# Causal part of the forgetting masks added on GpSimd behind the output gate, on diagonal blocks only, with the gate's factor made during the projection and a new order of the A/C stage

## The chip, the cores and the metric

The program runs on one core of a Trainium2 chip. The time is the device time of one execution in microseconds (us), from launch to end, the median of several runs. The core has five engines with a queue of instructions each: TensorE (PE in the profile, PEld for its weight loads), VectorE (DVE), ScalarE (ACT), GpSimd (POOL) and SyncE (SP), which here only issues the weight transfers. ACT's queue issues a few small transfers too. Engines wait for each other through semaphores, and every engine runs its own queue in order.

## The reference

Two layers of a decoder trunk on 256 tokens of width 1024, all in float32. Each layer is a half-step SwiGLU FFN, a mixer, and another half-step FFN. The mixer projects the normed tokens once and splits the result into three head groups that attend in parallel: A (4 query heads on one shared key head, keys chosen by an indexer's top 64), B (4 heads, plain causal at this length) and C (8 heads, with a bias from a cumulative forget gate, and a sigmoid output gate). Group C is what the change touches:

```python
def forgetting_attention(q, k, v, log_f):
    c = jnp.cumsum(log_f, axis=1).transpose(0, 2, 1)
    ...
        s = jnp.einsum('bqhd,bkhd->bhqk', qb, k).astype(jnp.float32) * scale
        s = s + cq[..., None] - c[:, :, None, :]
        s = jnp.where((key_pos[None, :] <= qpos[:, None])[None, None], s, -jnp.inf)
        p = jax.nn.softmax(s, axis=-1).astype(v.dtype)
...
    o_c = forgetting_attention(cq, ck, cv.reshape(B, S, C_HEADS, HEAD_DIM), log_f)
    o_c = o_c * jax.nn.sigmoid(cg)
    return jnp.concatenate([o_a, o_b, o_c], axis=-1) @ w_out
```

The term of a query's own row (`cq`) cancels in the softmax, so the kernel adds only the key's term.

## The kernel before

Tokens lie in two tiles of 128 partitions. To keep float32 accuracy on a faster matmul type, each weight is split in a high part (ACT, L123, a cast) and a low part (DVE, L127, a subtraction); `W.pump` records one such pair, and a product is three matmuls (`mm3`, all on L309). A split that is finished frees its raw buffer, and SP then issues the next 1 MB of weights (L97).

**The mixer** first runs the projection: eight column chunks (`CHUNKS`: iq, ib, b, a, ck, cq, cv, cg), each summed in two PSUM banks of the pool `gu` (four banks). Between the chunks' steps, `run_side` records the work that was put on a list with `at_step(n, ...)`: rotary, norms, the indexer's scores, top-k rounds, and the whole of group B. The last chunk, cg, holds the output gate. At step 32 the mask of group A (`amask`, L851 to L855, DVE) is made from the top-k scores. Group C's norms (`c_norm`, L707, four products of 128x512 on POOL) are recorded at step 25.

**The masks of group C** are four tiles of two heads each, `fmask[0..3]`, 128 x (2 x 384): a query tile's key columns are laid out as block 0 (query tile 0, keys 0 to 127), block 1 (query tile 1, keys 0 to 127) and block 2 (query tile 1, keys 128 to 255). Each is filled by a transfer that copies the heads' row of cumulated gates to all partitions (`spread`, L893, on ACT's queue); then `add_causal(j)` (L897, POOL) adds the tile `causal`, which is -1e30 above the diagonal in blocks 0 and 2 and zero in block 1. The first two lie in a tile named fmask, the third in gmask, the fourth in `spare`, a buffer that becomes free only when the projection has read its last input. `spare` holds also the gate `sg` and `cT`, group C's transposed queries and keys. The adds for j = 0, 1, 2 are recorded at step 28, the fourth at the end of `post_cg`.

**The gate**: `post_cg` makes `hr` = half the token norm (L1005, DVE, a 128x2 instruction), then the tanh of each token tile from the cg banks with `hr` as its scale (L1011, ACT), issues the fourth `spread`, and lets POOL turn tanh into a sigmoid (L1014, two instructions).

**The A/C stage** follows the projection. Its order is written out in `AC_ORDER`; each word records one step for all engines, so it sets the order in every queue:

- `c`, `C`, `g`, `G` + j: PE transposes queries and keys of C's head pair j (4 transposes, L1188) into a bank and ACT (small letter) or DVE (capital) copies it to `cT` (L1189). c and C use banks of the pool `acc`, g and G use `gu` banks.
- `s` + i: PE's scores of head pair i (0 and 1 are group A, 2 to 5 are C) into two `gu` banks.
- `m` + i: DVE adds the mask and finds the row's minimum (L1048, two pieces, each with a short read of its result); heads 0 to 3 are A, 4 to 11 are C, so m4 and m5 read fmask[0], m6 and m7 fmask[1], m8 and m9 gmask, m10 and m11 spare.
- `e`: ACT's exponentials (L1059). `d`: DVE divides by the row sum (L1065 and two L1067; group A only). `f`, `F`: PE's three transposes of the probabilities (L1072), copied by ACT or DVE (L1074).
- `v`, `o`: values (PE) and outputs to be projected. `h`: half of one block of the output projection, six matmuls. `w`: one weight split.

The stage ends where `tail` transposes the new trunk for the next norm (L344).

Of the kernel before, what the change touches and what calls it, by code (L numbers as in the profile page):

```python
# [10 lines left out]
F32 = mybir.dt.float32  # L11
# [3 lines left out]
ALU = mybir.AluOpType  # L15
# [3 lines left out]
P = 128  # L19
# [16 lines left out]
DOWN_LAG = 4  # L36
OUT_TAIL = 3
AC_ORDER = """
c0 C1 s0 s1 m1 h m0 e1 e0 m2 e2 c3 m3 d0 d1 h s2 d2 m4 s3 h e3 e4 f1 m6 h f0 m7 f2 m5 d3 f3 F4 e5 v0
v1 o0 G2 o1 e6 F5 h s4 e7 s5 m8 m9 e8 m10 h m11 e9 f6 v2 F7 f9 h w F8 e11 w o2 h e10 v3 F11 v4 f10 h  # L40
o4 o3 w v5 w h w
""".split()
HALVES_AHEAD = 2
WARM = 6
BRIDGE = 3
B_TURN, A_ROPE, B_STEP, A_ROOT, A_TURN, SUMS_STEP, MASK_STEP, ADD_STEP = 18, 18, 20, 22, 27, 23.7, 27.5, 28


CHUNKS = [
# [98 lines left out]
def kernel(ctx: ExitStack, tc: tile.TileContext, x, ffn1_norm, ffn1_w_gate, ffn1_w_up, ffn1_w_down,  # L148
# [9 lines left out]
    sm = ctx.enter_context(tc.tile_pool(name="sm", bufs=4))  # L158
# [6 lines left out]
    V, A, G, T = nc.vector, nc.scalar, nc.gpsimd, nc.tensor  # L165
# [131 lines left out]
    causal = cp.tile([P, 3 * P], F32, name="causal")  # L297
# [379 lines left out]
    def mixer(l, norm, nxt):  # L677
# [3 lines left out]
        def at_step(n, fn):  # L681
            side.append((n, next(count), fn))
# [7 lines left out]
        def heads(ap, n):  # L690
            return ap.rearrange("p (h d) -> p h d", h=n)
# [33 lines left out]
        def evac(dst, ps, t, scale=None):  # L725
            A.activation(dst, ps, AF.Copy, scale=norm.r[:, t:t + 1])
# [21 lines left out]
        st = {}  # L748
# [17 lines left out]
        def post_ib(ps):  # L766
# [119 lines left out]
            at_step(MASK_STEP, mask_tiles)  # L886
            at_step(SUMS_STEP, cumsum)
            at_step(SUMS_STEP + 1, forget_rows)
            at_step(ADD_STEP, lambda: [add_causal(j) for j in range(3)])

        def spread(m, h):
            rows_ = st["fd"][h:h + m.shape[1]]
            A.dma_start(m, bass.AP(tensor=rows_.tensor, offset=rows_.offset, ap=[[0, P]] + list(rows_.ap)))  # L893

        def add_causal(j):
            m = st["fmask"][j]
            G.tensor_tensor(m, m, causal[:, None, :].to_broadcast([P, 2, 3 * P]), op=ALU.add)  # L897

        def post_a(ps):
            ss = sm.tile([P, 2, 5], F32, name="ssa", tag="ss")  # L900
# [98 lines left out]
        def post_cv(ps):  # L999
            for t in range(2):  # L1000
                evac(va[t][:, :, 0:64], heads(ps[t], 8), t)

        def post_cg(ps):
            hr = sm.tile([P, 2], F32, name="hr", tag="hr")
            V.tensor_scalar(hr, norm.r, 0.5, None, op0=ALU.mult)  # L1005
            spare = xp.tile([P, 4096], F32, name="spare", tag="xhl")
            st["cT"] = spare[:, :2048].rearrange("p (h c s) -> p h c s", h=4, c=2)
            sg = spare[:, 2048:3072].rearrange("p (t d) -> p t d", t=2)
            st["fmask"].append(spare[:, 3072:3840].rearrange("p (h c) -> p h c", h=2))
            for t in range(2):  # L1010
                A.activation(sg[:, t], ps[t], AF.Tanh, scale=hr[:, t:t + 1])  # L1011
            spread(st["fmask"][3], 6)
            for t in range(2):
                G.tensor_scalar(sg[:, t], sg[:, t], 0.5, 0.5, op0=ALU.mult, op1=ALU.add)  # L1014
            add_causal(3)
            st["sg"] = sg


# [118 lines left out]

        oT = {}
        posts = dict(iq=post_iq, ib=post_ib, a=post_a, b=post_b, ck=post_ck, cq=post_cq, cv=post_cv, cg=post_cg)
        for name, cols in CHUNKS:  # L1140
            n = sum(c[1] for c in cols)
            ps = [bank("gu") for _ in range(2)]
            for u in range(4):
                w = W.take()
# [38 lines left out]
        def c_T(j, copy, b=None):  # L1183

            b = bank("gu") if b is None else b
            for c, src in enumerate((cq, ck)):
                for t in range(2):
                    T.transpose(b[:, c * S + t * P:c * S + (t + 1) * P], src[t][:, 2 * j:2 * j + 2], ident)  # L1188
            copy(cT[:, j], b.rearrange("p (c s) -> p c s", c=2))  # L1189

        def qk_ac(kind, h):
            if kind == "A":
# [4 lines left out]
        scores, masks, exps, divide, flip, values, outT = run_heads(hs, qk_ac, "gu")  # L1197
        run = dict(h=lambda i: next(halves), w=lambda i: W.pump(), m=masks, e=exps, d=divide,
                   s=lambda i: scores(2 * i), f=flip, F=lambda i: flip(i, V.tensor_copy),
                   c=lambda i: c_T(i, A.copy, acc[2 + i % 2]), C=lambda i: c_T(i, V.tensor_copy, acc[2 + i % 2]),  # L1200
                   g=lambda i: c_T(i, A.copy), G=lambda i: c_T(i, V.tensor_copy),
                   v=lambda i: values(2 * i + 1) if i < 2 else [values(2 * i + e) for e in range(2)],
                   o=lambda i: outT(i)())
        for word in AC_ORDER:
            run[word[0]](int(word[1:] or 0))
        return tail(acc, oT, OUT_ORDER[8 - OUT_TAIL:], 1.0, nxt, lambda: outT(len(hs) // 2 - 1)())
# [2 lines left out]
    def before_mixer(l):  # L1209
        if l == 0:  # L1210
            V.memset(causal[:, P:2 * P], 0.0)
            for t in range(2):
                V.tensor_scalar(causal[:, 2 * t * P:(2 * t + 1) * P], future, NEG, None, op0=ALU.mult)
        mixer_tables(l)
# [8 lines left out]
    norm = Norm(0, 0)  # L1223
    turn_gains()
    for l in range(DEPTH):
        norm = ffn(norm, lambda: Norm(1, l), lambda: before_mixer(l), l == 0)
        norm = mixer(l, norm, lambda: Norm(2, l))
        norm = ffn(norm, (lambda: Norm(0, l + 1)) if l + 1 < DEPTH else None)
# [35 lines left out]
```

## Time and profile before

| | |
|---|---|
| median of 3 runs | 1031.35 us (1031.28 to 1031.7) |
| the profiled execution's own time | 1029.86 us |
| its span, first to last instruction | 1027.5 us |
| mean granted TensorE clock | 0.997 |
| DVE busy | 809.1 us (79%) |
| ACT busy | 582.7 us (57%) |
| POOL busy | 161.5 us (16%) |
| A/C stage, layer 1: 284.61 (first L1188) to 328.85 (L344) | 44.24 us |
| A/C stage, layer 2: 793.72 to 837.96 | 44.24 us |

The page's rows give busy time as an average over the span. A row of a timeline has the start in us from the span's first instruction, the duration in us, the engine, the line, the operation, output<-inputs, the shape and the count of instructions merged; a bracket at its end is the idle time of the engine before it and who ended that. A matmul's duration overlaps its successor's, so PE's times are taken from one start to the next. Other engines' successive starts overlap by about a tenth of a microsecond too.

### The profile page before, as it was taken

The page shows a single profiled execution, that of the slowest core. Times are in us where ns is not written, and L with a number is a line of the kernel's source. Part 1 is how long each engine was busy: PE and PEld are TensorE (multiplying, and loading weights), DVE is VectorE, ACT ScalarE, POOL GpSimd, SP SyncE. Part 2 cuts the span into 40 slices and gives each one's busy share as a digit, 9 for nine tenths or more (in the row PEclk, how much of TensorE's full clock was granted, in tenths as well). Part 3 has the DMA queues.
Part 4 walks back from the last instruction along what each step waited for, and adds up shares of the span by engine and source line. Part 5 has one row for each costly group of instructions (what it writes and reads, how often), then busy time and mean ns, then how long its engine had stood idle before and what let it go on. Part 6 is the DMA issues. An engine that isn't in the chain of part 4 may idle for free.

```text
span 1027.5 us, 14846 instructions
## 1 busy us (share of the span) xinstructions
PE 1016.6 (99%) x5524; PEld 872.8 (85%) x5524; DVE 809.1 (79%) x1516; ACT 582.7 (57%) x1048; POOL 161.5 (16%) x185
## 2 busy tenths in 40 slices
PE   9999999999989999999999999999999999999998
PEld 8888888888868888888888888888887788888887
DVE  6978778789977877777888777787899778777776
ACT  6655555667645655555465555556775555555552
POOL 2003000166820000000000110002678100000000
PEclk9999999999999999999999999999999999999999
DMA  9674656555622464645645564755456134464731
GB/s 325 222 246 159 214 184 198 177 197 180 226 82 83 136 233 152 218 170 206 198 164 191 186 216 152 246 178 184 165 201 214 57 124 159 169 217 153 239 130 41
DMA packets 131703, 184.77 MB, mean 180 GB/s; under 512 B 7152, under 2 KB 104752, under 8 KB 131632
## 3 DMA queue, kind: packets, MB, share of 16 engines
q1 hardware_dynamic: 130704, 180.66, 52.2%
q10 hardware_dynamic: 928, 3.18, 1.0%
q8 instruction: 43, 0.70, 0.3%
q14 instruction: 28, 0.23, 0.1%
HBM read 182.75 MB, written 1.07 MB: 179 GB/s over the span
## 4 chain that ended last, share of the span: by engine, by line
PE 96%; DVE 3%; issue 0%; ACT 0%; POOL 0%; DVEq 0%; ACTq 0%; POOLq 0%
PE ps_gu L309 63%; PE ps_acc L309 29%; DVE wl L127 2%; PE ps_acc L344 1%; PE ps_gu L1072 1%; DVE amask L853 0%; PE ps_acc L738 0%; DVE amask L851 0%; DVE score L846 0%; DVE m L844 0%; PE ps_acc L1072 0%; ACT spare L1011 0%; PE ps_gu L1115 0%; PE ps_acc L506 0%; PE ps_gu L1188 0%
## 5 line engine op out<-in xcount | busy, mean ns | idle before, releaser
L127 DVE TENSOR_TENSOR wl<-raw,wh 128x1024 fp32r<-128x1024 f32 (+2 forms) x342 | 421.6, 1243 | 25.2 <-ACT wh L123 25.1
L123 ACT CAST wh<-raw 128x1024 fp32r<-128x1024 f32 (+2 forms) x341 | 342.4, 1036 | 12.9 <-PE ps_gu L309 11.0
L309 PE MATMUL ps_gu<-xhl,wh 128*128 128x512 f32 x1408 | 330.2, 390 | 0.3 <-DVE xhl L336 0.3
L309 PEld LDWEIGHTS ps_gu<-xhl,wh 128*128 128x128 f32 x1408 | 262.8, 188 | 54.1 <-issue 0.4
L309 PEld LDWEIGHTS ps_gu<-xhl,wl 128*128 128x128 f32 x1408 | 175.8, 192 | 4.1 <-DVE wl L490 0.2
L309 PE MATMUL ps_gu<-xhl,wl 128*128 128x256 f32 x1408 | 178.7, 284 | 0.0
L309 PE MATMUL ps_gu<-wh,xhl 128*128 128x512 f32 (+2 forms) x512 | 156.8, 379 | 0.0
L453 DVE TENSOR_TENSOR tmp<-ps_gu,tmp 128x256 f32<-128x256 f32 x176 | 72.9, 423 | 106.4 <-ACT tmp L452 106.2
L309 PE MATMUL ps_acc<-wh,hh 128*128 128x512 f32 (+1 forms) x352 | 137.3, 390 | 0.0
L309 PE MATMUL ps_acc<-wl,hh 128*128 128x512 f32 (+1 forms) x352 | 137.1, 389 | 0.0
L309 PE MATMUL ps_acc<-wh,hl 128*128 128x512 f32 (+1 forms) x352 | 136.6, 388 | 0.0
L452 ACT COPY tmp<-ps_gu 128x256 f32<-128x256 f32 x176 | 63.4, 371 | 92.1 <-PE ps_gu L309 91.8
L309 PEld LDWEIGHTS ps_gu<-wh,xhl 128*128 128x128 f32 x512 | 94.8, 188 | 16.2 <-issue 1.3
L467 ACT CAST hh<-tmp 128x256 fp32r<-128x256 f32 x80 | 32.6, 407 | 119.5 <-DVE tmp L464 119.5
L309 PE MATMUL ps_gu<-wl,xhl 128*128 128x512 f32 (+2 forms) x256 | 95.7, 374 | 0.0
L459 ACT ACTIVATE tmp<-tmp 128x256 f32<-128x256 f32 x88 | 36.8, 419 | 83.6 <-DVE tmp L457 83.2
L320 POOL TENSOR_TENSOR y_n<-msq,minus_half 128x2 f32<-128x2 f32 x6 | 7.0, 1168 | 491.4 <-DVE msq L319 491.4
L309 PEld LDWEIGHTS ps_acc<-wh,hl 128*128 128x128 f32 x352 | 66.2, 188 | 13.8
L309 PEld LDWEIGHTS ps_acc<-wh,hh 128*128 128x128 f32 x352 | 66.3, 188 | 12.6
L309 PEld LDWEIGHTS ps_acc<-wl,hh 128*128 128x128 f32 x352 | 66.3, 188 | 12.1
L309 PEld LDWEIGHTS ps_gu<-wl,xhl 128*128 128x128 f32 x256 | 48.2, 188 | 6.9
L333 ACT ACTIVATE xhl<-ps_acc,gT 128x256 fp32r<-128x256 f32 x48 | 19.0, 475 | 38.1 <-PE ps_acc L344 35.6
(230 smaller groups left out, 949.3 us busy)
## 6 DMA issues: line engine op xcount, KB each, us to landing
raw<-in_ffn_w_down_dram SPq DMA_DIRECT2D x44, 1024.0 KB, 5.0
raw<-in_ffn_w_gate_dram SPq DMA_DIRECT2D x42, 1024.0 KB, 6.6
raw<-in_ffn_w_up_dram SPq DMA_DIRECT2D x42, 1024.0 KB, 7.4
raw<-in_w_in_dram SPq DMA_DIRECT2D x24, 1024.0 KB, 5.2
raw<-in_w_out_dram SPq DMA_DIRECT2D x8, 1024.0 KB, 4.9
raw<-in_w_in_dram SPq DMA_DIRECT2D x4, 768.0 KB, 5.0
raw<-in_w_in_dram SPq DMA_DIRECT2D x4, 656.0 KB, 4.2
raw<-in_ffn_w_gate_dram SPq DMA_DIRECT2D x3, 512.0 KB, 6.4
```

What stands on the lines that cost most here:

```text
L123: self.nc.scalar.copy(hv, src)
L127: (engine or self.nc.vector).tensor_tensor(lv, self.srcs[self.n_low], hv.bitcast(F32), op=ALU.subtract)
L309: T.matmul(o, l, r, start=start, stop=stop, skip_group_check=True)
L320: G.tensor_tensor(y, dst, minus_half[:, :n], op=ALU.pow)
L333: A.activation(self.h[:, m], src, AF.Copy, scale=gT[:, self.col + m:self.col + m + 1])
L344: T.transpose(ps[:, i, t * P:(t + 1) * P], trunk[:, t, (2 * mp + i) * P:(2 * mp + i + 1) * P], ident)
L452: A.copy(o, ps[:, 1])
L453: V.tensor_tensor(o, ps[:, 0], o, op=ALU.add)
L459: A.activation(th, t_, AF.Tanh, scale=0.5)
L467: (V.tensor_copy if late else A.copy)(hh, t_)
L1072: T.transpose(b[:, j * P:(j + 1) * P], pj[i][:, j * P:(j + 1) * P], ident)
```

## The change

Four edits, the same in both layers. (1) `hr` is made at step 24 of the projection, not in `post_cg`. (2) The three adds of step 28 and the one of `post_cg` are taken out there and become words of the A/C order, `a0` to `a3`. (3) Each add works on blocks 0 and 2 alone, with a pattern of four dimensions, 512 elements of a partition where it was 768. (4) `AC_ORDER` is new. The old table began `c0 C1 s0 s1 m1 h m0 e1 e0 m2 e2 c3 m3 d0 d1 h s2 d2 m4 s3 h`; the new one is in the diff, with the `a` words in it.

```diff
+G3 C1 c0 s0 s1 m0 a0 h a3 e0 a2 m2 m3 m1 e2 h e1 d2 d0 e3 g2 d1 d3 s2 h m4 m5 f1 f0 e4 e5 h F2 F3 s4
+v0 m8 m9 a1 v1 o0 o1 f4 w s3 e8 e9 s5 h m10 h m7 m6 m11 F5 F8 e6 f9 v2 F6 h e11 e7 e10 f7 o2 v4 f10
...
-            at_step(ADD_STEP, lambda: [add_causal(j) for j in range(3)])
...
         def add_causal(j):
-            m = st["fmask"][j]
-            G.tensor_tensor(m, m, causal[:, None, :].to_broadcast([P, 2, 3 * P]), op=ALU.add)
+            m = st["fmask"][j].rearrange("p h (b c) -> p h b c", b=3)[:, :, 0:3:2]
+            both = causal.rearrange("p (b c) -> p b c", b=3)[:, None, 0:3:2].to_broadcast([P, 2, 2, P])
+            G.tensor_tensor(m, m, both, op=ALU.add)
...
+        hr = sm.tile([P, 2], F32, name="hr", tag="hr")
+        at_step(24, lambda: V.tensor_scalar(hr, norm.r, 0.5, None, op0=ALU.mult))
+
         def post_cg(ps):
-            hr = sm.tile([P, 2], F32, name="hr", tag="hr")
-            V.tensor_scalar(hr, norm.r, 0.5, None, op0=ALU.mult)
...
-            add_causal(3)
+            st["add"] = add_causal
...
-                   o=lambda i: outT(i)())
+                   o=lambda i: outT(i)(), a=st["add"])
```

POOL's queue at the end of layer 1's projection, before (-) and after (+); the first rows are group C's norms, the L1014 or L1015 rows the gate:

```order
 L707 TENSOR_TENSOR ck_130<-ck_130,y_c 128x512
 L707 TENSOR_TENSOR cq_128<-cq_128,y_c 128x512
-L897 TENSOR_TENSOR fmask<-fmask,causal 128x768 x2
-L897 TENSOR_TENSOR gmask<-gmask,causal 128x768
-L1014 TENSOR_SCALAR spare<-spare 128x512 x2
-L897 TENSOR_TENSOR spare<-spare,causal 128x768
+L1015 TENSOR_SCALAR spare<-spare 128x512 x2
+L897 TENSOR_TENSOR fmask<-fmask,causal 128x2x2x128
+L897 TENSOR_TENSOR spare<-spare,causal 128x2x2x128
+L897 TENSOR_TENSOR gmask<-gmask,causal 128x2x2x128
+L897 TENSOR_TENSOR fmask<-fmask,causal 128x2x2x128
```

The three adds that stood ahead of the gate now stand behind it, in the order fmask[0], spare, gmask, fmask[1]; the second of them needs the last transfer.

DVE's queue at the same place, before; `amask` is group A's mask, `ps_acc` the bank of C1:

```order
L127 TENSOR_TENSOR wl<-raw,wh 128x1024
L851 TENSOR_SCALAR amask<-score_2310 128x128
L853 SCALAR_TENSOR_TENSOR amask<-score_2309,cst 128x128
L853 SCALAR_TENSOR_TENSOR amask<-score_2310,cst 128x128
L855 TENSOR_SCALAR amask<-amask 128x384
L127 TENSOR_TENSOR wl<-raw,wh 128x1024
L1005 TENSOR_SCALAR hr<-y_n 128x2
L1189 COPY spare<-ps_acc 128x512
L1048 ISA tmp,nm<-ps_gu,amask,minus_a 128x128
```

And after; the row with `ps_gu` is G3's copy:

```order
L127 TENSOR_TENSOR wl<-raw,wh 128x1024
L851 TENSOR_SCALAR amask<-score_2311 128x128
L853 SCALAR_TENSOR_TENSOR amask<-score_2310,cst 128x128
L853 SCALAR_TENSOR_TENSOR amask<-score_2311,cst 128x128
L855 TENSOR_SCALAR amask<-amask 128x384
L127 TENSOR_TENSOR wl<-raw,wh 128x1024
L1190 COPY spare<-ps_gu 128x512
L1190 COPY spare<-ps_acc 128x512
L1049 ISA tmp,nm<-ps_gu,amask,minus_a 128x128
```

`hr` is gone from this place, and G3's copy stands there.

PE's queue after, at its first transposes of probabilities: the last three transposes of g2, s2 (`spare`), the third h (`wh,oh` opens each of its halves), and f1 with f0 (L1073):

```order
L1189 MATMUL ps_gu<-ident,cq_128 128x128
L1189 MATMUL ps_gu<-ident,ck_129 128x128
L1189 MATMUL ps_gu<-ident,ck_130 128x128
L309 MATMUL ps_gu<-spare 128x128 x2
L309 MATMUL ps_gu<-spare 128x256 x2
L309 MATMUL ps_acc<-wh,oh 128x512
L309 MATMUL ps_acc<-wl,oh 128x512
L309 MATMUL ps_acc<-wh,ol 128x512
L309 MATMUL ps_acc<-wh,oh 128x512
L309 MATMUL ps_acc<-wl,oh 128x512
L309 MATMUL ps_acc<-wh,ol 128x512
L1073 MATMUL ps_gu<-ident,p 128x128 x6
```

Ahead of them stand twelve transposes (G3, C1, c0), s0, s1 and two h; before, there were eight transposes (c0, C1) ahead of s0. With G3 in a `gu` bank, the two banks of s0 are now one that the chunk cv left and the one that G3's copy leaves, and the two of s1 are those of the gate. Before, s0 had cv's two banks and s1 the gate's two.

More of the change, by code (lines that the diff above doesn't have):

```diff
@@ L38 @@
 AC_ORDER = """
-c0 C1 s0 s1 m1 h m0 e1 e0 m2 e2 c3 m3 d0 d1 h s2 d2 m4 s3 h e3 e4 f1 m6 h f0 m7 f2 m5 d3 f3 F4 e5 v0
-v1 o0 G2 o1 e6 F5 h s4 e7 s5 m8 m9 e8 m10 h m11 e9 f6 v2 F7 f9 h w F8 e11 w o2 h e10 v3 F11 v4 f10 h
-o4 o3 w v5 w h w
+G3 C1 c0 s0 s1 m0 a0 h a3 e0 a2 m2 m3 m1 e2 h e1 d2 d0 e3 g2 d1 d3 s2 h m4 m5 f1 f0 e4 e5 h F2 F3 s4
+v0 m8 m9 a1 v1 o0 o1 f4 w s3 e8 e9 s5 h m10 h m7 m6 m11 F5 F8 e6 f9 v2 F6 h e11 e7 e10 f7 o2 v4 f10
+h w v3 w w f11 h o4 o3 v5 w h
 """.split()
@@ L45 @@
 BRIDGE = 3
-B_TURN, A_ROPE, B_STEP, A_ROOT, A_TURN, SUMS_STEP, MASK_STEP, ADD_STEP = 18, 18, 20, 22, 27, 23.7, 27.5, 28
+B_TURN, A_ROPE, B_STEP, A_ROOT, A_TURN, SUMS_STEP, MASK_STEP = 18, 18, 20, 22, 27, 23.7, 27.5
 CHUNKS = [
```

## The prediction

> **What bounds the kernel now.** I read the page, the waits of PE, then the A/C stage of layer 1 engine by engine in the timeline, with the granted clock of its stretches, and last layer 2's.
>
> ```profile
> PE 1016.6 (99%) x5524; PEld 872.8 (85%) x5524; DVE 809.1 (79%) x1516; ACT 582.7 (57%) x1048; POOL 161.5 (16%) x185
> PE ps_gu L309 <- ACT spare L1011: 6.4, 2, 3.2
> PE ps_gu L309 <- POOL minus_half L191: 1.0, 1, 1.0
> 284.60:289.60 5.00, 1.90 (x17) 1.32 (x15) 4.96 (x8) 0.66 (x2) 2.29 (x2) 1.00 0.00 0
> 289.60:294.40 4.80, 4.63 (x17) 3.23 (x18) 4.45 (x25) 3.70 (x15) 1.21 (x2) 0.64 0.80 264
> ```
>
> PE is busy for 99% of the span, so only what PE waits for, or runs slowly, can be won. The second row (who waited for whom: us in total, times, longest) is a large wait: twice 3.2 us for the gate's tanh, once in each layer. The next is the largest beside it. The other two are stretches of layer 1 (busy time of PE, PEld, DVE, ACT, POOL, then the clock, the share of the DMA engines and their GB/s): the wait lies in the first, and in the second the granted clock is 0.64. The wait is paid twice, as idle time and as a clock lost afterwards: 4.80 x (1 - 0.64) = 1.7 us.
>
> PE's timeline shows the sum:
>
> ```profile
> 284.61 0.38 PE L1188 MATMUL ps_acc<-ident,cq 128*128 128x128 f32 x2
> 285.57 0.93 PE L309 MATMUL ps_gu<-akT,aqT 64*128 64x128 f32 x8
> 289.68 1.69 PE L309 MATMUL ps_gu<-akT,aqT 64*128 64x128 f32 x8 [3.18 <-ACT spare L1011]
> 294.50 0.49 PE L309 MATMUL ps_acc<-wh,oh 128*128 128x512 f32 x1
> 296.08 1.58 PE L309 MATMUL ps_gu<-spare 64*128 64x128 f32 x16
> 297.59 0.50 PE L309 MATMUL ps_acc<-wh,oh 128*128 128x512 f32 x1
> 303.68 0.44 PE L1188 MATMUL ps_gu<-ident,cq 128*128 128x128 f32 x2
> 304.17 0.49 PE L1072 MATMUL ps_gu<-ident,p 128*128 128x128 f32 x3
> ```
>
> From 284.61 to 294.50 PE took 9.89 us for eight transposes, s0 and s1, one h and four transposes. At full clock, from starts of the same work: 0.96 (284.61 to 285.57), 1.51 for two s (296.08 to 297.59), 1.58 for one h (294.50 to 296.08), 0.49 (303.68 to 304.17), together 4.54. So **5.35 us are lost in a layer**. Layer 2 repeats it (793.72 to 803.65, 9.93 us):
>
> ```profile
> 793.72 0.38 PE L1188 MATMUL ps_acc<-ident,cq 128*128 128x128 f32 x2
> 803.65 0.49 PE L309 MATMUL ps_acc<-wh,oh 128*128 128x512 f32 x1
> ```
>
> Why the tanh is late stands in DVE, POOL and ACT:
>
> ```profile
> 280.73 2.68 DVE L127 TENSOR_TENSOR wl<-raw,wh 128x1024 fp32r<-128x1024 f32 x1
> 283.34 1.86 DVE L851 TENSOR_SCALAR amask<-score 128x128 f32<-128x128 f32 x1
> 285.12 2.12 DVE L853 SCALAR_TENSOR_TENSOR amask<-score,cst 128x128 f32<-128x128 f32 x2
> 287.27 0.36 DVE L855 TENSOR_SCALAR amask<-amask 128x384 f32<-128x384 f32 x1
> 287.55 1.22 DVE L127 TENSOR_TENSOR wl<-raw,wh 128x1024 fp32r<-128x1024 f32 x1
> 288.68 0.16 DVE L1005 TENSOR_SCALAR hr<-y_n 128x2 f32<-128x2 f32 x1
> 280.50 4.62 POOL L897 TENSOR_TENSOR fmask<-fmask,causal 128x768 f32<-128x768 f32 x2
> 285.07 1.82 POOL L897 TENSOR_TENSOR gmask<-gmask,causal 128x768 f32<-128x768 f32 x1
> 288.94 0.69 ACT L1011 ACTIVATE spare<-ps_gu,hr 128x512 f32<-128x512 f32 x1 [5.80 <-DVE hr L1005]
> 289.52 0.68 ACT L1011 ACTIVATE spare<-ps_gu,hr 128x512 f32<-128x512 f32 x1
> ```
>
> ACT idled 5.80 us for `hr`, which queued on DVE behind the mask of group A. DVE itself crawled: the same L127 takes 1.22 at 287.55 and 2.68 at 280.73, and 128 columns of L851 take 1.86 where 384 of L855 take 0.36. The slow ones end where an add of POOL ends: L127 at 283.41; L851 at 285.20, the first two adds at 285.12; L853's pair at 287.24, the third add at 286.89. I read that as one rule: these two engines take turns, and a DVE instruction between SBUF tiles waits for one whole add of POOL.
>
> **The change, part by part.** *hr at step 24*: one instruction of 0.16, beside dense projection matmuls; 0. The tanh then waits for PE alone and runs at 285.0 and 285.6. *Adds out of step 28*: DVE loses 2.68 - 1.22, 1.86 - 0.36 and 2.12 - 2 x 0.36, 4.4 us together, and `hr`; instead of at 288.75 it is free at about 284.2, before G3 needs it. G3's four transposes end at 285.25 and its copy ends at about 285.95, when PE, after twelve transposes (1.5 x 0.96 = 1.44), reaches s0 at 286.05. The gate's banks are free for s1 at 286.3, before 286.8. So the whole 5.35 us goes at its place.
>
> What is late next: f1, the first transposes of probabilities. PE reaches them after 1.44 + 1.51 + two h (2 x 1.58) + g2 (0.49) + s2 (half of 1.51) + the third h (1.58) = 8.9, at **293.55**. They need DVE's d1, behind d2 and d0:
>
> ```profile
> 289.35 0.34 DVE L1048 CUSTOM_DVE_ANT_0 tmp<-ps_gu,amask,minus_a 128x128 f32<-128x128 f32 x1
> 290.02 0.34 DVE L1048 CUSTOM_DVE_ANT_0 tmp<-ps_gu,amask,minus_a 128x128 f32<-128x128 f32 x1
> 290.56 0.42 ACT L1059 ACTIVATE p<-tmp,nm 128x128 f32<-128x128 f32 x1
> 291.44 0.40 ACT L1059 ACTIVATE p<-tmp,nm 128x128 f32<-128x128 f32 x1
> 292.46 0.17 DVE L1065 RECIPROCAL sums<-sums 128x2 f32<-128x2 f32 x1
> 293.12 0.16 DVE L1065 RECIPROCAL sums<-sums 128x2 f32<-128x2 f32 x1
> ```
>
> One m costs 0.67, one e 0.88, one d 0.66 (start to start). s0 ends at 287.0, four m at 289.7, e0, e2, e1 at 288.2, 289.1, 290.3, so d2, d0, d1 end at 290.4, 291.0, 291.7: 1.85 us ahead of PE, if nothing disturbs them. But now the adds do:
>
> ```profile
> 288.98 0.33 ACTq L893 DMA_DIRECT2D spare<-fd  x1
> 289.71 1.21 POOL L1014 TENSOR_SCALAR spare<-spare 128x512 f32<-128x512 f32 x2 [2.83 <-ACT spare L1011]
> 294.40 1.84 POOL L897 TENSOR_TENSOR spare<-spare,causal 128x768 f32<-128x768 f32 x1 [3.49 <-DMA spare<-fd]
> 261.39 1.61 DVE L1067 TENSOR_SCALAR p<-p,sums 128x128 f32<-128x128 f32 x2
> 275.52 1.04 POOL L707 TENSOR_TENSOR cq<-cq,y_c 128x512 f32<-128x512 f32 x1
> 261.49 2.67 POOL L988 TENSOR_TENSOR cq<-cq,gc 128x512 f32<-128x512 f32 x2
> ```
>
> a0 runs at 287 beside masks that read PSUM (an m takes 0.34 at 290.02 with the gate's L1014 running): 0. a3 waits for its transfer, 294.40 - 288.98 = 5.4 us after an issue now at 285.0, so until 290.4, with a2 and a1 queued behind it on POOL. These three fall on d0 and d1. That a division is hit like the other DVE instructions, 261.39 shows: a pair took 1.61 beside POOL where 0.66 - 0.16 = 0.5 is usual. An add of 512 elements I take by length, 1.84 x 512/768 = 1.23; its bounds are 1.04 (the fastest 512-wide product on POOL, at 275.52, the nearest row) and 1.84 (if the cost sits in the instruction, not in the elements). Taking turns, three adds stand ahead of d1's second piece: 290.4 + 1.3 (d0, d1) + 3.7 - 0.2 (a reciprocal beside an add) = 295.2. **PE stalls 295.2 - 293.55 = 1.65 us.** For the add's length the Trainium skill ("GPSIMD Engine Reference", 2.1) gives a two-input floor of about 2.5 cycles an element; at its 1.2 GHz that is an estimate of 1.07 for 512 and 1.6 for 768. The trace has 1.84 for 768, so the row decides; by the page the stall would be 1.15 and the time 1 us lower.
>
> After f1 the trace of before shows no PE wait to the stage's end; the new order is untried there, and 0 to one exposed copy of 0.56 a layer is its bound; I take 0, since each wait there was covered and the stall gives DVE and ACT more lead:
>
> ```profile
> 303.20 0.56 DVE L1074 COPY pT<-ps_gu 128x384 f32<-128x384 f32 x1 [2.98 <-PE ps_gu L309]
> ```
>
> SP's next weight transfer goes with the L127 of 287.55, now 4 us earlier, just ahead of the fourth spread as before: 0. Adds on two thirds of the elements are worth nothing off the path beyond the above. Sum: 5.35 - 1.65 = 3.7 a layer, **7.4 us** in two.
>
> **The rivals.** (a) *Adds clear of the divisions*: if the transfer lands over 1.3 us later (it shared the DMA engines, at 0.80, with a weight transfer), d1 is through first. No stall: 10.7 us, 1020.6. For it, the margin is only this; against, 5.4 us was measured with the same weight transfer just ahead of it. (b) *Bigger stall, or the clock falls again*: adds at 1.84 make the stall 3.5 (gain 1.85 a layer, 1027.7); or 1.65 idle is enough to lower the clock, 1.7 more (gain 2.0, 1027.4). The trace shows waits of 1.0 and 3.2 us and nothing between, and only those of 3.2 are followed by a lowered clock. The Trainium skill ("TensorE: Matmul & The Clock Gate", Part 1) has the clock halved after at least one idle window of about 3.4 us. By that 1.65 us keeps the clock; here 3.18 was enough, so its figure is no sharp edge. (c) *The change doesn't move the wait*: s0 now needs G3's copy, which stands behind group A's mask on DVE. If DVE isn't freed by the adds' removal, it gets there at 288.7 as before and PE waits in s0 instead of s1: about 1031. Against: the uneven L127 rows. (d) *Slower*: the four-dimensional pattern makes the adds slow. At 2.4 each the stall is 1.65 + 3 x 1.17 = 5.2, past the idle that cost the clock, so 6.9 a layer, 1.5 more than now: 1034.5. It decides from adds of 1.9 (stall 3.65 plus 1.7 equals 5.35). Against: contiguous runs of 128 columns remain.
>
> **How the numbers follow.** The profiled execution took 1029.86 (span 1027.5), 1.5 below the median of 1031.35; 1029.86 - 7.4 = 1022.5, and with the 1.5 the median becomes **1024.0 us**. Chances: the forecast (1022 to 1026) 0.54, (a) 0.20, (b) 0.12, (c) 0.08, (d) 0.06. The range from 1020.0 (a, with half a microsecond) to 1028.2 (b, with a copy) leaves (c) and (d) out. A measurement tells 0.2%, 2.1 us, from no change: faster is below 1029.3, the forecast, (a) and (b), 0.86; same is (c), 0.08; slower (d), 0.06.
>
> **What would show it.** Right: `hr` off the waits, tanh at the projection's end, no half clock in the stage, L851 under 0.4; a new PE wait of 1 to 2.5 us for DVE's L1068 at f1, with pairs of L1068 of over 1 us while L897 runs; L897 near 1.23. Wrong: a wait of PE for L1190 (c), L897 over 1.9 (d), a clock below 1.00 in the stage (b), no wait at L1073 (a), or a new wait after the first transposes, which I put at 0.

## The result, and the profile after

The changed kernel takes **1021.88 us** (median of 4 runs, 1021.64 to 1022.57). Beside it the kernel before took 1031.53 us (1031.28 to 1031.7). The ratio is 0.9908, with a 95% interval from 0.9891 to 0.9925: 9.65 us less. The forecast was 1024.0 with a range from 1020.0 to 1028.2. The profiled execution took 1021.84 us, with a span of 1019.8, against 1029.86 and 1027.5 before.

The page's row of busy times after, and what PE waited for (us in total, times, longest):

```profile
PE 1013.7 (99%) x5524; PEld 871.2 (85%) x5524; DVE 803.5 (79%) x1516; ACT 583.5 (57%) x1048; POOL 154.4 (15%) x185
```

```profile
PE ps_gu L1073 <- DVE p L1068: 2.0, 2, 1.1
PE ps_gu L309 <- POOL minus_half L191: 1.0, 1, 1.0
```

Two stretches of layer 1 (busy time of PE, PEld, DVE, ACT, POOL, then clock, DMA share, GB/s):

```profile
285.06:290.00 4.94, 4.94 (x38) 4.04 (x37) 3.77 (x17) 3.79 (x12) 2.44 (x3) 1.00 0.86 298
290.00:294.50 4.50, 3.89 (x23) 2.56 (x21) 4.43 (x9) 2.30 (x9) 3.80 (x3) 1.00 0.01 2
```

The wait for the tanh is gone, and with it the half clock. In its place stands a smaller wait, at the transposes of f1 (L1073) for DVE's divisions (L1068), once in each layer. PE is solidly busy up to it. PE's timeline gives the stages: start, f1 and end, in layer 1 and then in layer 2.

```profile
285.06 0.38 PE L1189 MATMUL ps_gu<-ident,cq 128*128 128x128 f32 x2
295.02 1.03 PE L1073 MATMUL ps_gu<-ident,p 128*128 128x128 f32 x6 [1.13 <-DVE p L1068]
325.33 1.03 PE L344 MATMUL ps_acc<-ident,trunk 128*128 128x128 f32 x8
790.21 0.38 PE L1189 MATMUL ps_gu<-ident,cq 128*128 128x128 f32 x2
799.91 1.03 PE L1073 MATMUL ps_gu<-ident,p 128*128 128x128 f32 x6 [0.88 <-DVE p L1068]
830.22 1.03 PE L344 MATMUL ps_acc<-ident,trunk 128*128 128x128 f32 x8
```

| | before | after |
|---|---|---|
| A/C stage, layer 1 | 44.24 | 325.33 - 285.06 = 40.27 |
| A/C stage, layer 2 | 44.24 | 830.22 - 790.21 = 40.01 |
| between them | 464.87 | 464.88 |
| start of the first stage | 284.61 | 285.06 |

The stages are 3.97 and 4.23 us shorter, 8.20 together. The later start takes 0.45 back; I take it for no effect of the change, since in a second trace of the kernel before (below) the first stage starts at 285.04. That is 7.75 us, and the spans differ by 7.7. The medians differ by 9.65: most of the rest is found below, in the clock of the kernel before.

DVE's rows in layer 1, the first three where before stood 2.68, 1.86 and 2.12 us:

```profile
281.19 1.21 DVE L127 TENSOR_TENSOR wl<-raw,wh 128x1024 fp32r<-128x1024 f32 x1
282.32 0.21 DVE L851 TENSOR_SCALAR amask<-score 128x128 f32<-128x128 f32 x1
282.45 0.48 DVE L853 SCALAR_TENSOR_TENSOR amask<-score,cst 128x128 f32<-128x128 f32 x2
283.24 1.22 DVE L127 TENSOR_TENSOR wl<-raw,wh 128x1024 fp32r<-128x1024 f32 x1
285.70 0.69 DVE L1190 COPY spare<-ps_gu 128x512 f32<-128x512 f32 x1 [1.24 <-PE ps_gu L1189]
290.43 1.61 DVE L1068 TENSOR_SCALAR p<-p,sums 128x128 f32<-128x128 f32 x2
292.15 2.42 DVE L1068 TENSOR_SCALAR p<-p,sums 128x128 f32<-128x128 f32 x2
294.68 0.55 DVE L1068 TENSOR_SCALAR p<-p,sums 128x128 f32<-128x128 f32 x2
```

Group A's mask is back at its own speed, DVE waits for PE ahead of G3's copy (1.24 us idle), and the slowness has moved to two of the three pairs of divisions (d2, d0, d1 in this order). ACT and POOL show why:

```profile
285.26 0.69 ACT L1012 ACTIVATE spare<-ps_gu,hr 128x512 f32<-128x512 f32 x1 [1.67 <-PE ps_gu L309]
285.27 0.33 ACTq L892 DMA_DIRECT2D spare<-fd  x1
287.21 1.27 POOL L897 TENSOR_TENSOR fmask<-fmask,causal 128x512 f32<-128x512 f32 x1
290.62 1.27 POOL L897 TENSOR_TENSOR spare<-spare,causal 128x512 f32<-128x512 f32 x1 [2.14 <-DMA spare<-fd]
291.85 1.33 POOL L897 TENSOR_TENSOR gmask<-gmask,causal 128x512 f32<-128x512 f32 x1
293.14 1.27 POOL L897 TENSOR_TENSOR fmask<-fmask,causal 128x512 f32<-128x512 f32 x1
```

The tanh waits for PE alone. a3 waits for its transfer until 290.62, and a3, a2 and a1 then run back to back, until 294.41. d2's second half is through when a3 ends, d0's halves when a2 and a1 end, and d1 is free after that.

### The profile page after: what moved, and what is told of

It is laid out like the page before. It is cut to its first block, busy times and chain, and to the rows that moved or that the text cites. A ratio compares the mean times of both kernels' runs of the same rounds, so it can differ in the third digit from the quotient of the medians.

```text
span 1019.8 us, 14836 instructions
## 1 busy us (share of the span) xinstructions
PE 1013.7 (99%) x5524; PEld 871.2 (85%) x5524; DVE 803.5 (79%) x1516; ACT 583.5 (57%) x1048; POOL 154.4 (15%) x185
## 3 DMA queue, kind: packets, MB, share of 16 engines
q10 hardware_dynamic: 928, 3.18, 1.0%
HBM read 182.75 MB, written 1.07 MB: 180 GB/s over the span
## 4 chain that ended last, share of the span: by engine, by line
PE 98%; DVE 1%; POOL 0%; ACT 0%; issue 0%; POOLq 0%
PE ps_gu L309 66%; PE ps_acc L309 28%; PE ps_gu L1073 1%; PE ps_acc L344 1%; DVE p L1068 1%; PE ps_acc L738 1%; DVE tmp L1049 1%; PE ps_acc L1073 0%; POOL spare L1015 0%; PE ps_acc L506 0%; PE ps_gu L1116 0%; ACT spare L1012 0%; PE ps_acc L371 0%; DVE sums L1066 0%; PE ps_acc L872 0%
## 5 line engine op out<-in xcount | busy, mean ns | idle before, releaser
L127 DVE TENSOR_TENSOR wl<-raw,wh 128x1024 fp32r<-128x1024 f32 (+2 forms) x342 | 416.3, 1228 | 24.7 <-ACT wh L123 24.6
L309 PEld LDWEIGHTS ps_acc<-wl,hh 128*128 128x128 f32 x352 | 66.3, 188 | 12.2
## 6 DMA issues: line engine op xcount, KB each, us to landing
raw<-in_ffn_w_down_dram SPq DMA_DIRECT2D x44, 1024.0 KB, 5.1
raw<-in_ffn_w_gate_dram SPq DMA_DIRECT2D x42, 1024.0 KB, 6.8
raw<-in_ffn_w_up_dram SPq DMA_DIRECT2D x42, 1024.0 KB, 7.5
raw<-in_w_in_dram SPq DMA_DIRECT2D x24, 1024.0 KB, 5.5
raw<-in_w_out_dram SPq DMA_DIRECT2D x8, 1024.0 KB, 4.9
raw<-in_ffn_w_gate_dram SPq DMA_DIRECT2D x3, 512.0 KB, 6.5
```

The source lines that it names most:

```text
L127: (engine or self.nc.vector).tensor_tensor(lv, self.srcs[self.n_low], hv.bitcast(F32), op=ALU.subtract)
L309: T.matmul(o, l, r, start=start, stop=stop, skip_group_check=True)
```

## The experiments

**The theories.** T (turns): DVE's instructions between SBUF tiles wait for a whole add of GpSimd; the adds of step 28 held up group A's mask and all behind it, and in the changed kernel three adds, queued behind the one that needs the last transfer, stand on the divisions that f1 needs. Rivals: R1, hr's place in DVE's queue is what matters. R2, the new order brings the gain. R3, the stall at f1 is DVE's own pile of masks and divisions. R0, the wait only moves. Each of the four edits was made alone on the kernel before, each was undone alone in the changed kernel, the adds were put in another order, and the kernel before was traced once more.

### hr alone, on the kernel before

```diff
+        hr = sm.tile([P, 2], F32, name="hr", tag="hr")
+        at_step(24, lambda: V.tensor_scalar(hr, norm.r, 0.5, None, op0=ALU.mult))
...
         def post_cg(ps):
-            hr = sm.tile([P, 2], F32, name="hr", tag="hr")
-            V.tensor_scalar(hr, norm.r, 0.5, None, op0=ALU.mult)
```

> The kernel before with one edit: hr at step 24. Theory T (turns): what held DVE was the three adds, hr only stood behind that; the tanh now runs when the projection ends (about 285.0 and 285.6 in layer 1), s1 no longer waits, but group A's mask, one L127 and C1's copy still end at about 289.4, so the first mask addition of a score is 3 us later than in the changed kernel and PE waits for it at the first instruction that needs a bank which a mask frees (c3's transposes, reached at about 288.6, released at 290.1: 1.5 us a layer). Gain 2 x (5.35 - 1.5) = 7.7, about 1023.8. Rival R1 (only hr's place in the queue matters): all of 5.35 a layer goes, about 1020.8. Rival R0 (DVE's lateness is the whole of it): the wait only moves, about 1031.

Measured: 1028.05 us (1025.57 to 1029.08), ratio 0.9959 (0.9944 to 0.9974). PE's waits:

```profile
PE ps_acc L1189 <- DVE spare L1190: 4.5, 2, 3.0
```

The tanh is on time and s1 no longer waits. But c3's transposes wait for C1's copy on DVE, which still stands behind the slowed mask: 3.0 us in layer 1, 1.4 in layer 2, where 1.5 was expected in both. The L127 behind the mask and the fourth add of GpSimd show the difference, first in layer 1, then in layer 2:

```profile
289.39 1.80 POOL L897 TENSOR_TENSOR spare<-spare,causal 128x768 f32<-128x768 f32 x1
289.41 2.87 DVE L127 TENSOR_TENSOR wl<-raw,wh 128x1024 fp32r<-128x1024 f32 x1
797.76 1.21 DVE L127 TENSOR_TENSOR wl<-raw,wh 128x1024 fp32r<-128x1024 f32 x1
797.80 2.85 POOL L897 TENSOR_TENSOR spare<-spare,causal 128x768 f32<-128x768 f32 x1 [0.17 <-DMA spare<-fd]
```

With the tanh early, the fourth add comes early too and meets L127. In layer 1 the add is ahead by 0.02 us and L127 waits for it; in layer 2 L127 is ahead by 0.04 and the add waits. So the turns go both ways, and the one that starts first holds up the other. In layer 1 a stretch at half clock follows the wait (the profiled execution's clock is 0.998; the others record 0.996 to 0.998). R1 falls, since most of the time comes back as another wait, and so does R0. I had the place right, but not this collision nor the clock: 1028.05 stands where 1023.8 was expected.

### The adds moved, alone

```diff
-            at_step(ADD_STEP, lambda: [add_causal(j) for j in range(3)])
...
-            add_causal(3)
+            for j in (0, 3, 2, 1):
+                add_causal(j)
```

> The kernel before with one edit: all four adds recorded behind the gate, in the order 0, 3, 2, 1, over all 768 columns; hr and the order of the stage as before. T: L127 back at 1.22, L851 and L853 under 0.4 and 0.8, DVE free by 284.2, hr done in time although it stands where it stood, tanh at about 285.0; the 5.35 us goes. In the old order d0 and d1 come through at 289.1 to 290.4, before the transfer for the fourth add lands (290.4), so the adds fall on d2 and a bank comes free late, 0 to 0.7 us at f1. Gain 9.3 to 10.7, about 1021.5. R1 (hr's place matters): the tanh stays late, about 1031. Rival R2 (the new order brings the gain): about 1031 or slower.

Measured: 1027.53 us (1026.18 to 1028.47), ratio 0.9955 (0.9939 to 0.9970). The timeline of layer 1, of DVE, then PE:

```profile
282.22 0.21 DVE L851 TENSOR_SCALAR amask<-score 128x128 f32<-128x128 f32 x1
284.28 0.16 DVE L1004 TENSOR_SCALAR hr<-y_n 128x2 f32<-128x2 f32 x1
290.56 3.79 DVE L1067 TENSOR_SCALAR p<-p,sums 128x128 f32<-128x128 f32 x2
294.45 1.89 DVE L1067 TENSOR_SCALAR p<-p,sums 128x128 f32<-128x128 f32 x2
296.95 0.90 PE L1072 MATMUL ps_gu<-ident,p 128*128 128x128 f32 x3 [2.92 <-DVE nm L1048]
```

The first half of T holds: the mask is quick, hr is done at 284.4 from its old place, and the wait for the tanh is gone. My forecast of what comes next failed: d1 starts at 290.56, just as the adds start, and its two halves catch two of them (3.79 us), d2 the third. m4, which frees a bank for f1, comes 2.92 us late, and about as late in layer 2. In the profiled execution the clock falls behind both waits (0.997). So more than half of the gain is lost again, 1027.53 where about 1021.5 was expected, and by the same turns.

### Whole adds in the changed kernel

```diff
         def add_causal(j):
-            m = st["fmask"][j].rearrange("p h (b c) -> p h b c", b=3)[:, :, 0:3:2]
...
+            m = st["fmask"][j]
+            G.tensor_tensor(m, m, causal[:, None, :].to_broadcast([P, 2, 3 * P]), op=ALU.add)
```

> The changed kernel with its adds over all 768 columns again. T: three adds of 1.84 where three of 1.27 stand on the divisions, so PE's stall at f1 grows from 1.0 to 1.0 + 3 x 0.57 = 2.7 us a layer: 1021.9 + 3.4 = 1025.3; if 2.7 us idle are enough to halve the clock for a stretch, 3.4 more, 1028.7. Rival R3 (the stall is DVE's own pile of masks and divisions, the adds add nothing): no change, 1021.9.

Measured: 1026.72 us (1026.37 to 1028.99), 4.84 more than the changed kernel. PE's waits:

```profile
PE ps_gu L1072 <- DVE p L1067: 5.4, 2, 2.7
```

And two stretches of 3.41 us in its layer 2, with the clock in the third column from the right:

```profile
800.43:803.84 3.41, 0.70 (x5) 0.31 (x4) 3.34 (x7) 0.00 (x0) 2.38 (x2) 1.00 0.00 0
803.84:807.25 3.41, 3.41 (x12) 2.73 (x12) 1.54 (x10) 2.34 (x6) 0.00 (x0) 0.51 0.00 0
```

The stall grew to 2.7, as T says; R3, which expects no change, falls. The clock fell in layer 2 but not in layer 1, with the same stall: 1025.3 for the stall and 1.7 for one lowered stretch make 1027.0.

### The add that waits put last

```diff
-G3 C1 c0 s0 s1 m0 a0 h a3 e0 a2 m2 m3 m1 e2 h e1 d2 d0 e3 g2 d1 d3 s2 h m4 m5 f1 f0 e4 e5 h F2 F3 s4
-v0 m8 m9 a1 v1 o0 o1 ...
+G3 C1 c0 s0 s1 m0 a0 h a2 e0 a1 a3 m2 m3 m1 e2 h e1 d2 d0 e3 g2 d1 d3 s2 h m4 m5 f1 f0 e4 e5 h F2 F3 s4
+v0 m8 m9 v1 o0 o1 ...
```

> The changed kernel with the adds in the order a0, a2, a1, a3: the one that waits for its transfer stands last on GpSimd. T: a2 and a1 then run right behind a0, at about 288.5 to 291.0, while DVE adds masks to scores in PSUM, and only the end of a1 and a3 (to about 292.3) fall on d2 and d0. d1 is through at about 293.5, ahead of PE's arrival at f1 (293.9): no stall, 1021.9 - 2.0 = 1019.9. R3 (DVE's own pile): unchanged, 1021.9. A third way: DVE's mask additions read an SBUF tile too, and if they take turns with the adds, the masks end up to 1.3 us later and the stall stays or grows: 1021.9 to 1023.

Measured: **1019.46 us** (1019.38 to 1019.72), ratio to the kernel before 0.9877 (0.9862 to 0.9891). It beats both kernels. The timeline of layer 1, of POOL, DVE and PE:

```profile
288.56 1.32 POOL L897 TENSOR_TENSOR gmask<-gmask,causal 128x512 f32<-128x512 f32 x1
289.83 1.30 POOL L897 TENSOR_TENSOR fmask<-fmask,causal 128x512 f32<-128x512 f32 x1
291.08 1.28 POOL L897 TENSOR_TENSOR spare<-spare,causal 128x512 f32<-128x512 f32 x1
290.56 1.95 DVE L1068 TENSOR_SCALAR p<-p,sums 128x128 f32<-128x128 f32 x2
293.28 0.55 DVE L1068 TENSOR_SCALAR p<-p,sums 128x128 f32<-128x128 f32 x2
285.19 0.38 PE L1189 MATMUL ps_gu<-ident,cq 128*128 128x128 f32 x2
293.87 0.82 PE L1073 MATMUL ps_gu<-ident,p 128*128 128x128 f32 x6
324.03 1.03 PE L344 MATMUL ps_acc<-ident,trunk 128*128 128x128 f32 x8
```

Only d2 is hit (1.95; d0 takes 0.55), d1 is through at 293.8, and f1 follows without a wait. The adds beside the mask additions, which read PSUM, cost nothing. The stage takes 324.03 - 285.19 = 38.84 us, the 44.24 - 5.35 = 38.89 that the prediction gives for a stage with no loss. In layer 2 it is 38.83.

### The adds back at step 28, the rest as changed

```diff
-G3 C1 c0 s0 s1 m0 a0 h a3 e0 a2 m2 m3 ...
-v0 m8 m9 a1 v1 o0 o1 ...
+G3 C1 c0 s0 s1 m0 h a3 e0 m2 m3 ...
+v0 m8 m9 v1 o0 o1 ...
...
+            at_step(28, lambda: [add_causal(j) for j in range(3)])
```

> The changed kernel with the three adds a0, a1, a2 back at step 28 of the projection (over blocks 0 and 2, 1.27 each), a3 alone behind the gate; hr early and the new order stay. T: three adds of 1.27 hold DVE for about 3.0 us (4.4 x 1.27/1.84), so G3's copy ends at about 288.1 instead of 286.4 and PE waits for it at s0, 1.7 us a layer; only a3 is left beside the divisions, no stall at f1. 1.7 in place of 1.0: 1021.9 + 1.4 = 1023.3. The rival (c) of the prediction as it stood there (adds of 1.84): a wait of about 3 us and a lowered clock, about 1028 to 1031. R1 (hr's place is what matters): no wait at s0, and without the stall at f1 about 1019.9.

Measured: 1027.54 us (1024.05 to 1027.7). PE's waits:

```profile
PE ps_gu L309 <- DVE spare L1191: 4.2, 2, 2.1
```

The wait moves to s0 for G3's copy, as in the prediction's third rival, and f1 has none. It is 2.1 us, not 1.7. Five of six executions record a clock of 0.997 and take 1027.5 to 1027.7; the sixth records 1.0 and takes 1024.05. I had left the clock out; without it, 1023.3 was near.

### The old order, the rest as changed

```diff
-G3 C1 c0 s0 s1 m0 a0 h a3 e0 a2 m2 m3 m1 e2 h e1 d2 d0 e3 g2 d1 d3 s2 h m4 m5 f1 f0 e4 e5 h F2 F3 s4
...
+c0 C1 s0 s1 m1 h m0 a0 a3 a2 a1 e1 e0 m2 e2 c3 m3 d0 d1 h s2 d2 m4 s3 h e3 e4 f1 m6 h f0 m7 f2 m5 d3 f3 F4 e5 v0
...
```

> The changed kernel with the old order of the A/C stage (the adds as words a0 a3 a2 a1 ahead of e1). T: as in the run with the adds alone moved, where three adds of 1.84 stood on d1 and d2 and a bank for f1 came 2.92 us late; with 1.27 each 1.7 less, so 1.2 us at f1. About as the changed kernel: 1022.2, within a microsecond; the new order by itself brings nothing. R2 (the order brings the gain): 1027 or more.

Measured: 1021.97 us (1021.79 to 1022.43), the changed kernel's time. PE's waits, again at f1:

```profile
PE ps_gu L1073 <- DVE nm L1049: 2.8, 2, 1.6
```

So the order as such brings nothing; R2 falls on this side. The old order with the waiting add last was not run.

### Blocks 0 and 2 alone, on the kernel before

```diff
-            m = st["fmask"][j]
-            G.tensor_tensor(m, m, causal[:, None, :].to_broadcast([P, 2, 3 * P]), op=ALU.add)
+            m = st["fmask"][j].rearrange("p h (b c) -> p h b c", b=3)[:, :, 0:3:2]
...
+            G.tensor_tensor(m, m, both, op=ALU.add)
```

> The kernel before with one edit: the adds work on blocks 0 and 2 alone, in their old places. T: DVE stands behind three adds of 1.27 instead of 1.84, hr comes 1.7 us earlier, PE's wait for the tanh shrinks from 3.18 to 1.5 us, and that is too short for the lowered clock: 5.35 becomes 1.5 a layer, about 1030 - 7.7 = 1022.3 by the profiled execution, 1022 to 1024 by the median. Rival (DVE's slowness does not go by the adds' length): the wait stays near 3.2, about 1031.

Measured: 1024.40 us (1023.38 to 1026.79), ratio 0.9939 (0.9921 to 0.9956). PE's waits:

```profile
PE ps_gu L309 <- ACT spare L1012: 3.1, 2, 1.6
```

The timeline of layer 1, a row of DVE and one of POOL:

```profile
283.54 1.31 DVE L851 TENSOR_SCALAR amask<-score 128x128 f32<-128x128 f32 x1
284.72 1.28 POOL L898 TENSOR_TENSOR gmask<-gmask,causal 128x512 f32<-128x512 f32 x1
```

L851, 1.86 us beside whole adds, takes 1.31, about one short add. The wait fell from 3.18 to 1.55, as worked out. The four executions record a clock of 1.0 (1023.38 and 1023.57), 0.998 (1025.23) and 0.997 (1026.79): steps of about 1.6 us for each lowered stretch. A wait of 1.55 is thus at the edge.

### The kernel before, once more

No edit.

> The kernel before, once more, for its clock. In each trace with a wait of 2.2 us or more, the clock falls to half for one stretch of 3.41 us. The profiled execution of before has two such stretches, mean clock 0.997 (2 x 3.41 x 0.5 / 1028 = 0.0033); most other executions of it record 0.995, which is three. Theory C1: the third lies at the same wait, right behind the first stretch of one layer, and costs about the 1.5 us by which those executions are longer; it goes with the wait, so it belongs to the change's gain. C2: it lies elsewhere (the program's start, an FFN) and the changed kernel has it as well; against this, the changed kernel's executions all record 1.0.

Measured: 1030.79 us (1029.77 to 1032.68) beside 1031.04 of its twin. This profiled execution records 0.995. Three stretches of 3.41 us around layer 1's wait:

```profile
286.01:289.42 3.41, 0.92 (x9) 0.52 (x8) 3.38 (x6) 0.05 (x1) 1.31 (x1) 1.00 0.00 1
289.42:292.83 3.41, 2.72 (x9) 1.92 (x10) 2.67 (x14) 3.41 (x12) 1.20 (x2) 0.50 0.56 167
292.83:296.25 3.42, 3.42 (x11) 2.73 (x10) 3.31 (x12) 1.08 (x6) 1.72 (x1) 0.50 0.71 255
```

C1 holds in this trace: two lowered stretches stand back to back at the one wait, and layer 2 has one more. The second of them costs less than 1.5 us: layer 1's stage takes 45.23 us (285.04 to 330.27) instead of 44.24, and the whole execution 1.2 more than the first profiled one. Of the 25 executions of the kernel before in this round, ten record 0.997 and take 1029.77 to 1030.91, and fifteen record 0.994 or 0.995 and take 1030.67 to 1032.68. The profiled execution of before, with 0.997, was thus by chance one of the shorter ones; the changed kernel's four all record 1.0.

### hr back in post_cg; the new order alone

The first is the changed kernel, the second the kernel before, each with one edit.

```diff
-        at_step(24, lambda: V.tensor_scalar(hr, norm.r, 0.5, None, op0=ALU.mult))
...
         def post_cg(ps):
...
+            V.tensor_scalar(hr, norm.r, 0.5, None, op0=ALU.mult)
```

> The changed kernel with hr made in post_cg again. T: with the adds out of step 28 DVE comes to hr at about 284.4, before the projection's last matmul, so the tanh starts when it did, at 285.3: no change, 1021.9. R1 (hr's place in the queue brings the gain): the wait for the tanh comes back, 1025 or more.

```diff
-c0 C1 s0 s1 m1 h m0 e1 e0 m2 e2 c3 m3 d0 d1 h s2 d2 m4 s3 h e3 e4 f1 m6 h f0 m7 f2 m5 d3 f3 F4 e5 v0
...
+G3 C1 c0 s0 s1 m0 h e0 m2 m3 m1 e2 h e1 d2 d0 e3 g2 d1 d3 s2 h m4 m5 f1 f0 e4 e5 h F2 F3 s4
...
```

> The kernel before with one edit: the new order of the A/C stage (without the words of the adds, which stay at step 28 and behind the gate). T: G3's copy stands behind hr on DVE and ends at about 289.5, so PE waits 3.4 us for it at s0 where it waited 3.2 for the tanh at s1, and loses one or two stretches of the clock as before: 1031, within a microsecond or two. R2 (the order brings a part of the gain): 1028 or less.

Measured: 1022.25 us (1021.72 to 1022.58) for hr, no change beside 1021.88; 1030.14 us (1028.84 to 1030.87), ratio 0.9984 (0.9975 to 0.9994), for the order. PE's waits in the second:

```profile
PE ps_gu L309 <- DVE spare L1189: 6.0, 2, 3.0
```

With the adds gone from step 28, hr can stand in either of its two places. With them there, the new order only exchanges the wait for the tanh for one for G3's copy.

Alone, the four edits bring 3.6 (hr), 4.1 (adds moved), 6.6 (shorter adds) and 1.4 us (order), each against the median beside it. Undone alone, they cost 0.4, 5.7, 4.8 and 0.1; the 0.4 and the 0.1 lie within the spread of the runs. What carries the change is where the adds run and how long they are.

## Why the prediction was right, and where it was off

- **hr for 0, adds out of step 28 frees DVE by 4.4 us, all 5.35 goes.** Right. DVE is ready before G3's copy; the stage without a stall takes 38.84 where 38.89 was worked out. That hr costs nothing is right, but it also brings nothing beside the other edits, which the prediction left open. One reading was off: the L127 of 280.73 doesn't end with an add. The first add ends at 282.33, L127 runs behind it until 283.41, and the second add waits for that and takes 2.82 us. The sum did not need this half of the rule.
- **The stall at f1: 1.65 us.** The mechanism was right and the size was off. By the stages it is 40.27 - 38.84 = 1.43 and 40.01 - 38.83 = 1.18; the listed idle time, 1.13 and 0.88, leaves out above all that the six transposes behind it take 1.03 us instead of 0.82. The adds were 1.27 to 1.37 in the two layers (1.23 forecast). Two terms were too large: the transfer landed 5.35 us after its issue, as forecast, but the issue came 0.21 after the stage's start instead of 0.4, so the pile began earlier; and I added the divisions (1.3) to the adds (3.7) in series, while the three adds ran back to back and d2's and d0's halves went beside them. Only d1 was left behind the last add. The estimate from the Trainium skill ("GPSIMD Engine Reference", 2.1), 1.07 us for an add, would have given a stall of 1.15, nearer to the result, but for a wrong reason: no add was under 1.26.
- **After f1: 0.** Right; the page names no other wait of PE.
- **"With the 1.5 the median becomes 1024.0."** This step failed. By profiled executions the forecast was 1022.5 and the result 1021.84, 0.7 off, which is the stall. The other 1.5 I carried over as an offset between the profiled execution and the median. Most of it was a cost of the wait itself: most executions of before record a clock that is lower by one more stretch, and the second trace of before shows that stretch at the wait. It costs 1.0 to 1.2 us there, and it went with the wait. The last 0.3 to 0.5 stays open.
- **The rivals.** (a) did not happen, but the order of the adds in the run with a3 last makes its case: 10.7 us forecast, 12.2 measured against the median beside it, again with the 1.5. (b) is real in both parts: longer adds gave 2.7 us of stall (3.5 forecast) and a lowered clock, and the kernel before with short adds shows that a wait of 1.55 can lower it. The forecast stall stood at the edge of that; the true one stays clear of it. (c) appears when the adds are put back at step 28. (d) is refuted: 1.27 for an add of four dimensions.

## What to carry to other kernels

When GpSimd and VectorE both work between SBUF tiles, ask of each GpSimd instruction which VectorE instruction it will meet and who waits for that one; moving it out of the way of one may put it in the way of another, as it did here. In an in-order queue, the instruction that waits for a transfer should go last if nothing needs its result sooner; here it held two others back until they met the worst moment. An execution that is shorter than the median may have met the clock better, and then the difference belongs to the wait that costs the clock, not to an offset that stays.

## What the runs showed of the hardware

- **The clock goes by stretches of 3.41 us on a grid.** Every lowered stretch within the program lasts 3.41 us or twice that. In the second trace of before they start at 289.42 and 801.42, 512.0 us or 150 such lengths apart. The grid's place differs from execution to execution: in the first trace of before, the lowered stretch of layer 1 starts at 290.86. So one kernel takes several times: 1023.4, 1025.2 and 1026.8 us in the run with short adds on the kernel before.
- **It takes less than a whole idle stretch.** Half clock followed stretches in which PE was busy for 0.70 us (whole adds, layer 2), 0.92 (before, second trace) and 1.76, in the kernel before with short adds, in the stretch ahead of its lowered one:

```profile
286.74:290.15 3.41, 1.76 (x14) 0.91 (x10) 3.19 (x13) 2.09 (x6) 1.21 (x2) 1.00 0.25 67
```

  It did not follow either of two stretches of the run with whole adds. Its lowered stretch of layer 2 starts at 803.84, and 149 lengths earlier a border lies at 295.30, in the middle of layer 1's stall of 2.7 us; on both sides PE is busy for over 2 us:

```profile
291.89:295.30 3.41, 2.03 (x12) 1.09 (x8) 3.37 (x4) 0.44 (x1) 3.41 (x3) 1.00 0.00 0
295.30:298.71 3.41, 2.08 (x12) 1.74 (x13) 3.23 (x15) 1.34 (x4) 0.73 (x1) 1.00 0.00 0
```

  The run with the new order alone shows the same more sharply. Both its layers have a wait of 3.0 us. In layer 1 it falls on two stretches, and the clock stays (the lowered stretches of layer 2 begin at 796.84, 149 lengths behind the border at 288.26):

```profile
284.84:288.25 3.41, 1.94 (x15) 1.53 (x13) 3.38 (x5) 0.00 (x0) 2.33 (x2) 1.00 0.01 2
288.26:291.67 3.41, 1.89 (x15) 1.50 (x16) 3.11 (x11) 2.40 (x6) 1.21 (x2) 1.00 0.36 84
```

  In layer 2 it falls almost whole on one, with 0.63 us busy, and the two lowered stretches follow. So where a wait meets the grid decides as much as its length.

  The Trainium skill ("TensorE: Matmul & The Clock Gate", Part 1) has a free-running window of 3413 ns, which agrees, and the clock halved after at least one idle window, where these runs need only about half a window idle. Why the stretch from 289.42 in the second trace of before (2.72 us busy, at half clock) was followed by another lowered one stays open; in the run with the adds moved alone, a lowered stretch from 296.29 with 2.75 us busy was followed by full clock.
- **The turns go both ways; the one that starts first holds up the other.** A division waits for a whole add, 1.27 to 1.84 us. The adds hardly notice the divisions, which are short: three adds in a row took 3.79 us, 1.26 each, with three halves of divisions between and beside them. But behind a long L127 an add of 1.84 takes 2.85 (hr alone, layer 2) or 2.82 (before, the second add of step 28). The mask additions, which read PSUM, met adds without a loss. The Trainium skill ("SBUF — State Buffer", "SBUF: two separate sides") describes a port pair that the two engines share and that the first to start locks for its whole instruction; the long rows of both engines agree with that.
